# A two-layer Mamba-2 and attention trunk on eight cores: from 512-token blocks in a hand-written order to phases over the whole sequence in a list-scheduled order

## The chip, the cores and the metric

One Trainium2 chip, two dies of four cores. The program runs on all eight cores; each core computes one of the eight sequences of the batch (2048 tokens of 1024 features), and there is no traffic between cores. The metric is the device time of the slowest core, in microseconds (us). Engines: PE does matmuls (PEld its weight loads), DVE is the vector engine, ACT the scalar engine, POOL the GpSimd, SP issues transfers.

The program has a second, slower state: in some executions the cores of one die get a lower clock and take some per cent longer. Runs in that state are marked slow below, and only fast runs are compared.

## The reference, cut to what matters

The lines are shortened and put together by hand; the shapes are the reference's own.

```python
def reference(x, ...):                        # x: (8, 2048, 1024) float32
    # layer 1
    h = rms_norm(x, a_norm)
    x = x + mamba2_mixer(h, ...)              # in-projection 1024 -> 6176, out-projection 2048 -> 1024
    x = x + conv_ffn(x, f_norm[0], ...)
    # layer 2: keys and values shared, from the stream after layer 1
    k, v = split(rms_norm(x, kv_norm) @ w_kv + b_kv);  k = rotary(rms_norm(k, k_norm), positions)
    q = rotary(rms_norm(rms_norm(x, b_norm) @ w_q + b_q, q_norm), positions)
    x = x + sliding_window_sink_attention(q, k, v, sinks) @ w_o + b_o   # 16 query heads, 4 kv heads of 64, window 128
    x = x + conv_ffn(x, f_norm[1], ...)
    return x

def mamba2_mixer(h, ...):
    z, xBC, dt = split(h @ in_proj)                       # 2048, 2048 + 1024 + 1024, 32
    xs, B, C = split(silu(causal_dwconv(xBC, conv_w, conv_b)))   # 4 taps
    dt = softplus(dt + dt_bias);  A = -exp(A_log)
    # per chunk of L tokens, 32 heads of 64, 8 groups of B and C with state 128:
    #   y  = (C B^T * exp(a_cum[l] - a_cum[s]), causal) @ (dt x)  +  (C @ state) * exp(a_cum)
    #   state = state * exp(a_cum[last]) + B^T @ (exp(a_cum[last] - a_cum) dt x)
    y = ssd_chunked(xs, dt, A, B, C) + xs * D
    return group_rms_norm(y * silu(z), gnorm, 8) @ out_proj

def conv_ffn(x, g, w_in, conv_w, conv_b, w_down):          # 1024 -> 2 x 2816 -> 1024
    gate, val = split(rms_norm(x, g) @ w_in)
    return (silu(causal_dwconv(gate, conv_w, conv_b)) * val) @ w_down   # 3 taps
```

## The kernel before

It walks over four blocks of 512 tokens. Each block passes all stages: transposes of the input, norm, in-projection with convolution, SSD scan in chunks of 256 tokens, gated norm, out-projection, FFN, attention, FFN, output. The residual is feature-major (`xT`, features on partitions), so the sum of squares of a norm runs over partitions and takes a matmul with ones. All weights are loaded anew for every block. Engines work in the order in which the program is written; a helper records each operation and adds the semaphores.

```python
    for b in range(NBLK):                       # 4 blocks of 512 tokens
        ...
        rms_stats(lambda c: xT[:, c, :], 8, ones, 1.0 / D)
        ...
        for t in INP_ORDER:                     # in-projection, 512 columns at a time
            ...
        for ck in range(2):                     # two chunks of 256
            items = [(g, hh) for g in range(8) for hh in range(4)]   # one head at a time: s1, s2, s3 below

    def rms_stats(src_fn, nch, lhs, scale):
        bk = bank()
        for c in range(nch):
            ...                                 # squares, by ACT and DVE in turn
            K.mm(ps[:, bk, :], lhs, sqb[:, c % 2, :], start=(c == 0), stop=(c == nch - 1))
        K.act(lnb[:], ps[:, bk, :], AF.Ln, bias=epsb[:, 0:1], scale=scale)
        K.act(rstd[:], lnb[:], AF.Exp, scale=-0.5)

    def conv_taps(dst_acc, src_ps, raw, ntap, wname_fn, bname):
        K.act(dst_acc, src_ps, AF.Identity, bias=bname, scale=wname_fn(ntap - 1))
        for k in range(ntap - 2, -1, -1):       # raw: a copy of the bank in SBUF, with the last tokens of the block before
            K.stt(dst_acc, raw[:, k:k + TB], wname_fn(k), dst_acc, OP.mult, OP.add)

            def s2(i):                          # one head of the scan: three exponents, two products
                ...
                K.act(Erow[:, r, :]..., pa4[:, :, 0, :], AF.Exp)
                K.act(Eb[:, r, 0:256], ps[:, ba, 128:384], AF.Exp, bias=nacum[:, tl0, h:h + 1])
                K.act(Eb[:, r, 256:384], ps[:, ba, 384:512], AF.Exp, bias=nacum[:, tl1, h:h + 1])
                K.tt(Wt[:, r, :], CBb[:, g % 2, :], Eb[:, r, :], OP.mult)
                K.tt(Cs[:, r, :], CT[:, g, c0:c0 + 256], Erow[:, r, :], OP.mult)

                    # attention: one 128-query tile of one kv head
                    K.mm(ps[:, bs_, :]..., kT[P0:P0 + 64, pi, kt * 128:(kt + 1) * 128], qT_v[P0:P0 + 64, pi, :, qs], ...)
                    ...
                        K.mm(ps[P0:P0 + 64, bo_, :], vtok[:, kt, g * 64:(g + 1) * 64], pt, start=first, stop=last)
                        K.mm(ps[P0:P0 + 64, bd_, :], ones[:, 0:64], pt, start=first, stop=last)   # the denominator
                                    ...
                                    K.add("dve", (lambda e: e.reciprocal(dtot, dtot)), [dtot], [dtot])
```

The softmax here doesn't subtract the row's maximum and nothing guards it: scores larger than these inputs give would overflow.

## Time and profile before

| | before |
|---|---|
| runs (us) | 2699.05, 2696.23, 2768.55 |
| Mamba front, four blocks | 918 us |
| gated norm and out-projection | 182 us |
| FFNs, with output | 1050 us |
| attention | 554 us |
| moved by transfers | 248.37 MB |

Read the run's spread first: the third run is 2.6% longer than the other two, so it counts as slow. The stage sums are those of the prediction, cut from the trace where the PE work changes. Next, the head of the profile page: span, busy time of each engine (share of the span, number of instructions), and busy tenths in 40 slices of the span; PEclk is the granted clock of PE in tenths.

```profile
span 2704.2 us, 36898 instructions; the slowest of 8 cores (2688.7 to 2704.2 us)
...
PE 2282.5 (84%) x10240; PEld 980.2 (36%) x10240; DVE 1690.0 (62%) x3101; ACT 1271.6 (47%) x2806; POOL 457.2 (17%) x740
...
PE   5877997889786799878978679987897867998799
...
DVE  5887465653688655655368865565536896556553
...
PEclk8988997689898889668989888966898988896789
...
DMA packets 409782, 248.37 MB, mean 92 GB/s; under 512 B 85104, under 2 KB 404720, under 8 KB 409584
```

The four blocks can be seen as a pattern of ten slices that repeats: DVE high (8) in the front of each block, PE at 9 in the FFNs, and the clock down to 6 or 7 in each attention. Nearly all of the 409782 packets are under 2 KB.

### The profile page before, as it was taken

What the parts mean: (1) busy time and instruction counts of PE and PEld (TensorE: products, weight loads), DVE (VectorE), ACT (ScalarE), POOL (GpSimd) and SP (SyncE); (2) the same over time, 40 slices, a digit from 0 to 9 for tenths busy, and PEclk for the clock granted to TensorE, in tenths of its full rate; (3) what the DMA queues carried; (4) which work ended last, traced back from release to release, by engine and by line L of the source; (5) the groups of instructions that cost most, each with busy time, mean ns of one, the idle gap of its engine ahead of it and who ended that gap; (6) DMA issues with size and microseconds to landing.
All of it is one profiled execution on the core that took longest, in us unless ns stands there. A gap on an engine that the chain in (4) does not pass through costs nothing.

```text
span 2704.2 us, 36898 instructions; the slowest of 8 cores (2688.7 to 2704.2 us)
## 1 busy us (share of the span) xinstructions
PE 2282.5 (84%) x10240; PEld 980.2 (36%) x10240; DVE 1690.0 (62%) x3101; ACT 1271.6 (47%) x2806; POOL 457.2 (17%) x740
## 2 busy tenths in 40 slices
PE   5877997889786799878978679987897867998799
PEld 2443342234343334223434433422343433342234
DVE  5887465653688655655368865565536896556553
ACT  4667334342666542424266654242426665424342
POOL 1211222011120112101112011310111201131010
PEclk8988997689898889668989888966898988896789
DMA  8922999099780499709978049970997804997196
GB/s 141 125 33 51 117 133 109 8 116 120 135 122 3 84 122 122 83 9 119 119 133 123 2 84 123 123 80 12 114 123 137 122 2 50 122 121 82 24 117 109
DMA packets 409782, 248.37 MB, mean 92 GB/s; under 512 B 85104, under 2 KB 404720, under 8 KB 409584
## 3 DMA queue, kind: packets, MB, share of 16 engines
q0 software_dynamic: 403968, 227.31, 67.4%
q1 hardware_dynamic: 5616, 18.72, 2.0%
q8 instruction: 89, 1.46, 0.2%
q14 instruction: 109, 0.89, 0.1%
HBM read 464.88 MB, written 8.39 MB: 175 GB/s over the span
## 4 chain that ended last, share of the span: by engine, by line
PE 72%; DVE 13%; ACT 8%; issue 6%; DMA 0%; DVEq 0%; ACTq 0%; POOL 0%; SPq 0%; POOLq 0%
PE ps_ps L286 70%; DVE sb_accb L315 3%; DVE sb_Wt L305 2%; PE ps_ps L290 1%; ACT sb_sqb L302 1%; DVE sb_sqb L305 1%; ACT sb_accb L302 1%; ACT sb_lnb L302 1%; DVE sb_xdb L305 1%; ACT sb_Eb L302 1%; DVE sb_hT L1028 1%; ACT sb_Erow L302 1%; DVE sb_xcT L305 1%; ACT L302 1%; ACT sb_rstd L302 1%
## 5 line engine op out<-in xcount | busy, mean ns | idle before, releaser
L286 PE MATMUL ps_ps<-sb_hT,sb_wring 128*128 128x512 bf16 (+1 forms) x4384 | 1020.2, 394 | 64.1 <-DVE sb_hT L315 34.9
L315 DVE SCALAR_TENSOR_TENSOR sb_accb<-sb_rawb,sb_cst,sb_accb 128x512 f32<-128x512 f32 x736 | 543.5, 751 | 305.3 <-ACT sb_accb L302 241.7
L286 PEld LDWEIGHTS ps_ps<-sb_hT,sb_wring 128*128 128x128 bf16 (+1 forms) x4384 | 438.5, 100 | 643.8 <-issue 163.9
L302 ACT ACTIVATE sb_rawb<-ps_ps 128x512 f32<-128x512 f32 (+1 forms) x428 | 254.1, 594 | 494.6 <-PE ps_ps L286 494.0
L286 PE MATMUL ps_ps<-sb_zsT,sb_wring 128*128 128x512 bf16 x1856 | 443.1, 392 | 20.9 <-DVE sb_zsT L315 15.6
L324 POOL DMA_DIRECT2D sb_wring<-f_w_in x176 | 154.2, 878 | 1008.6 <-PE ps_ps L286 1008.6
L286 PEld LDWEIGHTS ps_ps<-sb_zsT,sb_wring 128*128 128x128 bf16 x1856 | 184.6, 100 | 260.2 <-issue 56.6
L302 ACT ACTIVATE sb_accb<-ps_ps,sb_cst 128x512 f32<-128x512 f32 x304 | 236.6, 778 | 20.0 <-DVE sb_accb L305 20.0
L305 DVE TENSOR_TENSOR sb_xT<-sb_xT,ps_ps 128x512 f32<-128x512 f32 x96 | 64.9, 686 | 268.7 <-PE ps_ps L286 267.5
L302 ACT ACTIVATE sb_Eb<-ps_ps,sb_nacum 128x256 bf16<-128x256 f32 (+1 forms) x512 | 197.8, 467 | 0.0
L286 PE MATMUL ps_ps<-sb_sqb,sb_cm 128*128 128x512 bf16 x220 | 96.5, 483 | 95.4 <-DVE sb_sqb L305 47.4
L302 ACT ACTIVATE sb_sqb<-sb_xT 128x512 bf16<-128x512 f32 x64 | 40.7, 636 | 285.6 <-PE ps_ps L286 235.5
L286 PE MATMUL ps_ps<-sb_xcT,sb_wring 128*128 128x512 bf16 x640 | 156.3, 391 | 13.2 <-DVE sb_xcT L305 9.5
L286 PE MATMUL ps_ps<-sb_Wt,sb_xdb 128*64 128x256 bf16 (+1 forms) x512 | 90.6, 260 | 72.6 <-DVE sb_Wt L305 72.5
L286 PE MATMUL ps_ps<-sb_cm 128*128 128x128 bf16 (+1 forms) x636 | 150.0, 304 | 0.0
L302 ACT ACTIVATE sb_zsT<-ps_ps 128x512 bf16<-128x512 f32 (+1 forms) x96 | 50.8, 602 | 187.0 <-PE ps_ps L290 146.4
L302 ACT ACTIVATE sb_Erow<-ps_ps 128x256 bf16<-128x256 f32 x256 | 108.2, 423 | 57.0 <-PE ps_ps L286 41.5
L286 PE MATMUL ps_ps<-sb_AH,sb_cm 128*128 128x512 bf16 x256 | 108.5, 424 | 18.8 <-DVE sb_xtk L318 18.5
L305 DVE TENSOR_TENSOR sb_Wt<-sb_CBb,sb_Eb 128x384 bf16<-128x384 bf16 x256 | 112.5, 440 | 14.7 <-ACT sb_Eb L302 14.5
L302 ACT ACTIVATE sb_xtk<-sb_accb 128x512 bf16<-128x512 f32 x176 | 112.1, 637 | 10.4 <-DVE sb_accb L315 10.3
L324 POOL DMA_DIRECT2D sb_wring<-f_w_down x64 | 54.1, 845 | 339.1 <-PE ps_ps L286 339.1
L310 DVE TENSOR_SCALAR sb_hT<-ps_ps,sb_esink 128x128 f32<-128x128 f32 x128 | 36.0, 344 | 114.2 <-PE ps_ps L286 114.2
(131 smaller groups left out, 2559.5 us busy)
## 6 DMA issues: line engine op xcount, KB each, us to landing
sb_wring<-f_w_in POOLq DMA_DIRECT2D x176, 512.0 KB, 9.2
sb_wring<-a_in_proj POOLq DMA_DIRECT2D x48, 1024.0 KB, 12.3
sb_wring<-f_w_down POOLq DMA_DIRECT2D x32, 768.0 KB, 9.0
sb_wring<-f_w_down POOLq DMA_DIRECT2D x32, 640.0 KB, 8.2
sb_wring<-a_out_proj POOLq DMA_DIRECT2D x16, 1024.0 KB, 9.3
sb_xdb<-x SPq DMA_DIRECT2D x16, 512.0 KB, 10.5
sb_wring<-w_q POOLq DMA_DIRECT2D x64, 128.0 KB, 13.8
sb_wring<-w_o POOLq DMA_DIRECT2D x32, 256.0 KB, 14.6
```

Of the source, the lines that this page charges most:

```text
L286: return self.add("pe", lambda e: e.matmul(out, lhsT, rhs, start=start, stop=stop), [lhsT, rhs] + ([] if start else [out]), [out])
L290: return self.add("pe", lambda e: e.transpose(out, in_, ident), [in_, ident], [out])
L302: return self.add("act", lambda e: e.activation(out, in_, func, **kw), rd, [out])
L305: return self.add(eng, lambda e: e.tensor_tensor(out, in0, in1, op), [in0, in1], [out])
L310: return self.add(eng, lambda e: e.tensor_scalar(out, in0, s1, None, op0), rd, [out])
L315: return self.add("dve", lambda e: e.scalar_tensor_tensor(out, in0, scalar, in1, op0, op1), rd, [out])
L324: return self.add(queue, lambda e: e.dma_start(out=out, in_=in_), [in_], [out], dma_sem=sem)
L1028: K.add("dve", (lambda e: e.reciprocal(dtot, dtot)), [dtot], [dtot])
```

## The change

The intent is one of structure: run each stage over the whole sequence before the next begins, so that it is filled and drained once and its weights are read less often; keep the residual token-major, so that a norm's sum comes out of the squaring activation; work on 1024 columns per instruction; put four heads into one exponent tile; and leave the order of instructions on each engine to a list scheduler that has a cost for each operation. PSUM has eight banks of 512 columns: in the front, banks 0 to 3 are two pairs for the projections, 4 to 7 serve the scan. To evacuate a bank is to copy its contents to SBUF, so that it can be written again.

The diff replaces nearly every line; its core, with cuts marked by dots:

```diff
-NBLK = T // TB
-    for b in range(NBLK):
+    units = [(g, h) for g in range(8) for h in range(2)]      # one B/C group, half of the sequence
+    for i, (g, h) in enumerate(units):
+        if i + 1 < len(units):
+            P_unit(*units[i + 1])                             # projections and convolution of the next unit
+        S_unit(g, h)                                          # scan of this one
+    def S_unit(g, h):
+        arload(g, h)
+        for q in range(2):                                    # 512 tokens: the "piece" of the text below
+            S_head(g, h, q)
+            while tails:
+                S_tail(*tails.pop(0))
+            S_core(g, h, q)
+            tails.append((g, h, q))
 ...
     P_unit:
-        K.act(rawb[:, r, 3:3 + TB], ps[:, bk, :], AF.Copy)
-        conv_taps(acc, ps[:, bk, :], rawb[:, r, :], 4, lambda k: C(f"cw{k}", j), C("cb", j))
+            K.act(acc, pp, AF.Identity, bias=C("cb", j), scale=C("cw3", j))     # pp: two banks, 1024 columns
+            for s in (1, 2, 3):
+                K.stt(acc[:, s:1024], pp[:, 0:1024 - s], C(f"cw{3 - s}", j), acc[:, s:1024], OP.mult, OP.add)
+            K.act(dst, acc, AF.Silu)
 ...
     S_head: transposes of x, of B, and the B-C products, all in bank 7, each evacuated before the next
     S_core:
-                K.act(Erow[:, r, :]..., AF.Exp)
-                K.act(Eb[:, r, 0:256], ..., AF.Exp, bias=nacum[:, tl0, h:h + 1])
-                K.act(Eb[:, r, 256:384], ..., AF.Exp, bias=nacum[:, tl1, h:h + 1])
+            K.mm(bank(4), LTb[...][:, q, c, :], RTb[r][:]..., start=True, stop=False)   # 4 heads of 128 columns
+            K.act(e_[:]..., bank(4), AF.Exp)
+            K.tt(W[c][:], e_[:], CBB[r][:, c, :].unsqueeze(1).to_broadcast([128, 4, 128]), OP.mult)
+                K.mm(ps[:, 7, k * 256:(k + 1) * 256], BtB[r][:, c, :], xddB[r][:, c, :], start=True, stop=True)   # states
+                K.copy(prevB[c][:], pF, eng="pool")
+                K.tt(st..., pF..., cdec[...], OP.mult, eng="pool")
+                K.tt(pF, st, ps[:, 7, k * 256:(k + 1) * 256], OP.add)
     S_tail:
+        pb = ps[:, 7, :].bitcast(BF16)...                     # transposes of the gated output, then into yT
 ...
     norm:
-            K.mm(ps[:, bk, :], lhs, sqb[:, c % 2, :], start=(c == 0), stop=(c == nch - 1))
+            K.act(junk[i % len(junk)], xv, AF.Square, scale=1.0 / 32.0, accum=ssq[:, r, i:i + 1])
 ...
     attention:
-                    K.mm(ps[:, bs_, :]..., kT[P0:P0 + 64, ...], qT_v[P0:P0 + 64, ...], start=True, stop=False)
+                        K.mm(s4, kz[:, g, kt * 128:(kt + 1) * 128], qv[:, pi, :, qs], start=True, stop=False)   # zero-padded keys
-                        K.mm(ps[P0:P0 + 64, bd_, :], ones[:, 0:64], pt, start=first, stop=last)
+                        K.mm(bank(pav), vA[:, kt, g, :], P, ...)      # values with a half of ones: pav = 6 + half
-                                    K.add("dve", (lambda e: e.reciprocal(dtot, dtot)), [dtot], [dtot])
+                K.act(dt_[:], dt_[:], AF.Ln)
+                K.act(dt_[:], dt_[:], AF.Exp, scale=-1.0)
 ...
     order of each engine:
-            for op in self.ops[eng]:                          # as written
+        self.schedule()                                       # ready list by priority, costs per operation
+            if is_w: deps.add(last writer of the bank); deps.update(readers of the bank)    # PSUM: by whole bank
```

The lines ahead of a colon and the last line are shortened by hand; all others are the kernels' own.

## The prediction

> **What bounds the kernel now.** I first read the spans and clocks of the cores (all eight 2689 to 2704 us, dies at 0.874 and 0.876: an undisturbed run), then the chain that ended last (it names PE for 72%, matmuls of one helper line), then busy time by stage. The stages are cut where the PE work changes; the second of the four 512-token blocks is: Mamba front (norm, in-projection, convolution, SSD scan), gated norm and out-projection, first FFN, attention, second FFN.
>
> ```profile
> PE 72%; DVE 13%; ACT 8%; issue 6%; DMA 0%; DVEq 0%; ACTq 0%; POOL 0%; SPq 0%; POOLq 0%
> ```
> ```profile
> core 0: us, PE busy (x) PEld busy (x) DVE busy (x) ACT busy (x) POOL busy (x), PEclk, DMA share, GB/s
> 679.00:904.20 225.20, 174.45 (x988) 88.22 (x987) 186.95 (x406) 148.91 (x349) 37.66 (x94) 0.89 0.49 76
> 904.20:949.30 45.10, 36.84 (x148) 14.56 (x147) 17.91 (x28) 17.64 (x31) 5.72 (x7) 0.81 0.82 134
> 949.30:1077.40 128.10, 121.68 (x538) 52.88 (x536) 72.03 (x110) 49.26 (x119) 33.03 (x38) 0.95 0.99 121
> 1077.40:1221.00 143.60, 114.57 (x334) 32.77 (x332) 81.99 (x140) 52.39 (x83) 12.83 (x17) 0.68 0.48 52
> 1221.00:1355.00 134.00, 125.86 (x575) 57.01 (x574) 62.28 (x90) 50.95 (x124) 25.08 (x29) 0.95 0.94 116
> ```
> ```profile
> 1258.00:1292.00 34.00, 34.00 (x159) 15.41 (x158) 20.48 (x30) 19.10 (x49) 6.95 (x8) 1.00 1.21 151
> 1122.00:1156.00 34.00, 31.70 (x69) 6.32 (x68) 17.67 (x34) 10.79 (x18) 0.00 (x0) 0.57 0.04 5
> ```
> Read matmul counts, not busy shares. In the FFN 159 matmuls of 512 columns take 34.00 us: 0.2138 us each at clock 1.00, as tight as it gets. In the attention PE is also "busy" for 31.7 of 34 us but does 69 matmuls, at clock 0.57. In the Mamba front DVE is busy for 187 of 225 us (83%), PE is not dense: DVE sets the pace. So three stages have three limits. Over the four blocks they sum to 918 us front, 182 gate and out-projection, 1050 FFN (with output), 554 attention: 2704.
>
> ```profile
> L315 DVE SCALAR_TENSOR_TENSOR sb_accb<-sb_rawb,sb_cst,sb_accb 128x512 f32<-128x512 f32 x736 | 543.5, 751 | 305.3 <-ACT sb_accb L302 241.7 <-ACT sb_rawb L302 18.2 <-DVE sb_accb L315 0.5
> L302 ACT ACTIVATE sb_accb<-ps_ps,sb_cst 128x512 f32<-128x512 f32 x304 | 236.6, 778 | 20.0 <-DVE sb_accb L305 20.0
> L305 DVE TENSOR_TENSOR sb_xT<-sb_xT,ps_ps 128x512 f32<-128x512 f32 x96 | 64.9, 686 | 268.7 <-PE ps_ps L286 267.5 <-PE ps_ps L290 1.2
> L1028 DVE RECIPROCAL sb_hT<-sb_hT 128x512 f32<-128x512 f32 x24 | 80.5, 3353 | 2.5
> L302 ACT ACT_TABLE_LOAD x24 | 30.8, 1283 | 23.2 <-PE ps_ps L286 12.5 <-DVE sb_accb L315 6.2 <-DMA sb_cst<-cst 4.4
> ```
> These groups give the prices. From pairs of sizes (472 ns at 256 and 751 at 512 for the three-operand op, 415 and 686 for the two-operand op) I extrapolate to 1024 columns: about 1.29 us and 1.22 us; an activation with two pointer operands 1.20 us, a plain one 1.02 us.
>
> **What the skill says.** "TensorE: Matmul & The Clock Gate", Part 1, has the clock at half or full by recent activity, and warns of 13/16 once three cores of a die are dense. The first agrees (69 against 159 matmuls in 34 us; clock 0.57 against 1.00); the second does not show here: eight cores run dense FFNs at 1.00. "ScalarE: Activation LUTs", What ACT_TABLE_LOAD costs, says about 1283 ns for each change of set; the row above reads 1283. "Advanced Engine Details and Errata", VectorE Performance Modes, says GPSIMD and two-port vector instructions block each other; here, beside a POOL multiply, one bf16 product takes twice its time:
> ```profile
> 211.46 0.66 POOL L305 TENSOR_TENSOR sb_stmp<-sb_prevF,sb_cdec 128x256 f32<-128x256 f32 x1 [20.17 <-DVE sb_prevF L305]
> 211.56 0.77 DVE L305 TENSOR_TENSOR sb_Wt<-sb_CBb,sb_Eb 128x384 bf16<-128x384 bf16 x1
> 212.46 0.35 DVE L305 TENSOR_TENSOR sb_Wt<-sb_CBb,sb_Eb 128x384 bf16<-128x384 bf16 x1
> ```
>
> **The change part by part.** *PE work hardly shrinks.* Before: 7904 streams of 512 columns, 832 of 256, 1216 of 128 and some 270 fp32 transposes; at 0.2138 us per 512, about 1900 us. After, counted from its instructions: 7076 of 512, 1408 of 256, and some 2,300 of 128 or fewer (transposes in bf16): about 1785. Gone are the 220 norm sums and half of the SSD's exponent streams; the projections (5760 of 512) stay. So of the 2704 us, 800 is PE idle or cold, and it is there that the change must earn.
>
> *FFN.* 4224 matmuls x 0.2138 = 903 us before and after. Before, eight FFNs each open with a norm (squares, ones-matmul, Ln, Exp, eight scalings) with PE waiting: 1050 - 903 = 147 us lost. After, there are four half-sequence passes; the second half's norm is issued within the first half's gate stage. I count 256 transposes (14 us) and four starts, four gate-to-down and two end bubbles at about 5 us: 903 + 14 + 45 = 962. DVE there needs 441 us, so it stays hidden.
>
> *Mamba front.* In-projection 332 us and SSD 170 us of PE, plus 15. DVE by its prices: 192 convolution steps x 1.29 = 247, their edges 24, 128 masked products of 512 53, state updates 54, output products 132, scaled inputs 39, norm scalings 29, 12 for the other tile, evacuations about 30, tables, norms and dt about 55: 683 us in all. The same sum for the old block is 206 us against a union of 187, as independent neighbours overlap by some 84 ns; with the same 0.91 that is 620. The old front had 753. So the front stays DVE-bound and shrinks by less than a fifth. New costs: POOL now has 256 small state operations (135 us by 0.67 and about 0.4) against 64, so collisions: about 25 us. Table changes on ACT: the fixed instruction order has about 107 in the front against 12; 107 x 1.283 = 137 us, ACT then about 535, still under DVE. In the dense part of the old front DVE was 87% occupied (148.8 of 170 us). (620 + 25) / 0.87 = 741, plus about 20 before the first tiles are in: 760, against 918.
>
> *Gate and out-projection.* The group norm moves into the scan (counted above); the 512 matmuls, 110 us, stay, some 30 us of them beside the last scan unit, and a bubble follows for the first FFN norm, whose scratch lies under the last gated tiles: 85, against 182.
>
> *Attention.* Heads of 64 become full 128-row and 128-column operands (zero-padded keys, values with a ones half), which drops the 124 separate denominator streams; the 3.35 us reciprocals become Ln and Exp. Per block PE has 61 us, ACT 57, DVE 58. The value banks are single, so each query tile passes add, Ln, Exp, multiply before the next values: about 4.5 to 5 us each, 8 per block, about 38. With norm 5, projections of k, v, q 20, a chain of 8, output 14, less 3 of overlap: 82 to 90 per block, 355 in all against 554.
>
> Sum: 760 + 85 + 962 + 355 = 2162. As the list scheduler may overlap more across stages than I allowed, I shade this to 2140.
>
> *Weights.* Read twice or three times rather than four times, in long rows: DMA share, about 1.0 in the old FFN, should halve. No old wait is for weights, so this earns nothing directly.
>
> **The rivals.** (a) Dense PE trips the power limit. If FFN ran at 13/16, 962 would become about 1170, the total 2350. Against it: 1.00 in every dense FFN window; the slow run of 2768.55 us shows the state exists. (b) The front stalls in one PSUM bank: transposes, B-C products, states and output tiles share bank 7, about 14 us for each 512 tokens without contention, 20 with DVE queues, so 40 us per unit against DVE's 42. If they add rather than overlap, the front takes 850 and the total 2240. (c) Table changes make ACT the bound if each drags a drain with it: front 820. (d) The scheduler does much better than a hand order: DVE 95% occupied, front 690; attention 300, limited by PE and ACT; total about 2020. (e) Attention stays cold as now: the 96 attention streams of a block at 0.5 us rather than 0.21 add about 15 us a block, total 2200.
>
> **Range and chances.** (b), (c) and (e) lean up, (d) down; 2010 to 2290 covers all but (a). To miss 2% faster (2645) all gains but one would have to fail. Faster 0.97, same 0.02, slower 0.01.
>
> **What would show it.** Right: FFN stretches at clock 1.00 with about 159 matmuls per 34 us for over 900 us; DVE at 85% or more through the first 750 us with ACT at about 70%; about 110 table loads; attention near 88 us per block at a clock above 0.8; DMA share about 0.5. Wrong: a front under 700 or over 830; attention over 105 a block; FFN clock of about 0.81; PE waiting on bank 7's evacuations.

## The result, and the profile after

Ratios are computed as the mean time of one kernel's fast runs over that of the other's fast runs of the same rounds, so they are not quite the ratio of the medians, which take in slow runs too.

| | before | after |
|---|---|---|
| runs (us) | 2699.05, 2696.23, 2768.55 (slow), 2729.83 (state not on record) | 2172.00, 2170.62, 2186.64, 2227.78 (slow) |
| median | 2714.44 | 2179.32 |

Ratio of the fast runs 0.805, 95% interval 0.7988 to 0.8112: faster. In the slow run of after, the cores of die 1 took 2191 to 2227 us at clocks of 0.935 to 0.94, those of die 0 2168 to 2171 at 0.97. The profiled run is a fast one (2172.00 us, cores 2167.0 to 2170.9).

The head of the page of after, the same lines as for before, and its chain:

```profile
span 2170.9 us, 31606 instructions; the slowest of 8 cores (2167.0 to 2170.9 us)
...
PE 1927.3 (89%) x10808; PEld 943.2 (43%) x10808; DVE 1315.6 (61%) x2112; ACT 1055.7 (49%) x1635; POOL 372.2 (17%) x609
...
PE   2878888888888899899999999788888899999999
...
DVE  4888788878887751665235532767667665225532
...
PEclk9898999999999999999999999999999999999999
...
DMA packets 47851, 148.63 MB, mean 68 GB/s; under 512 B 9808, under 2 KB 11088, under 8 KB 47696
...
PE 73%; DVE 12%; issue 7%; ACT 4%; DMA 1%; POOL 1%; SPq 0%; DVEq 0%; ACTq 0%; POOLq 0%
```

PE is busy 355 us less, and the clock is at 9 tenths or more in all but two slices. The chain looks as before (PE 73%), which shows how little a share over the whole span says; the stages say more. Busy time by stage (columns as in the prediction's table), cut on the slowest core where the PE work changes: start, front, last scan piece, out-projection, first FFN, attention, second FFN; then 34 us each from the middle of the front, of an FFN gate stage, and of the attention:

```profile
core 1: us, PE busy (x) PEld busy (x) DVE busy (x) ACT busy (x) POOL busy (x), PEclk, DMA share, GB/s
0.00:68.00 68.00, 21.47 (x132) 12.23 (x133) 31.96 (x79) 28.09 (x49) 14.57 (x29) 0.92 0.73 185
68.00:737.00 669.00, 559.21 (x4158) 325.63 (x4157) 561.99 (x1018) 503.22 (x815) 125.79 (x254) 0.95 0.13 26
737.00:794.30 57.30, 54.09 (x400) 27.56 (x398) 39.74 (x81) 29.79 (x76) 20.07 (x40) 1.00 0.73 171
794.30:871.70 77.40, 77.40 (x359) 34.66 (x356) 15.82 (x23) 1.47 (x3) 7.38 (x14) 1.00 0.70 126
871.70:1345.60 473.90, 466.52 (x2244) 214.96 (x2244) 220.34 (x279) 130.64 (x144) 49.94 (x81) 0.99 0.43 74
1345.60:1695.60 350.00, 282.28 (x1285) 113.28 (x1282) 231.05 (x363) 244.02 (x430) 111.22 (x117) 0.96 0.36 63
1695.60:2170.90 475.30, 466.30 (x2241) 214.88 (x2240) 214.70 (x270) 118.43 (x121) 43.20 (x75) 0.99 0.47 89
476.00:510.00 34.00, 29.22 (x206) 15.48 (x204) 26.69 (x49) 24.89 (x43) 8.28 (x17) 0.95 0.10 18
1156.00:1190.00 34.00, 34.00 (x160) 15.41 (x158) 20.10 (x25) 10.77 (x11) 2.64 (x5) 1.00 0.44 75
1462.00:1496.00 34.00, 27.32 (x114) 9.62 (x113) 24.12 (x37) 28.77 (x55) 8.87 (x9) 1.00 0.33 63
```

| stage, us | before | predicted | after |
|---|---|---|---|
| Mamba front | 918 | 760 | 794.3 |
| gated norm and out-projection | 182 | 85 | 77.4 |
| FFNs, with output | 1050 | 962 | 949.2 |
| attention | 554 | 355 | 350.0 |
| sum | 2704 | 2162, shaded to 2140 | 2170.9 |

So attention gave the most (204 us), then the front (124), the gate and out-projection (105) and the FFNs (101). In the FFN 160 matmuls in 34 us against 159: the dense part is what it was, and the gain is in the norms and bubbles around it. In the attention window the clock is 1.00 and there are 114 matmuls where before had 69. In the front three engines are busy most of the time at once: of 669 us, PE is busy 84%, DVE 84%, ACT 75%.

The groups with the new prices and the new table loads (the first column after the count is busy time, then the mean in ns, then the idle time before):

```profile
L254 ACT ACT_TABLE_LOAD x110 | 141.1, 1283 | 56.2 <-PE ps L229 39.1
...
L269 DVE SCALAR_TENSOR_TENSOR acc_121<-ps,cst,acc_121 128x1023 f32<-128x1023 f32 (+2 forms) x96 | 122.3, 1274 | 6.0 <-ACT acc_121 L254 5.7
...
L254 ACT ACTIVATE facc_188<-ps,cst 128x1024 f32<-128x1024 f32 x44 | 53.0, 1204 | 146.5 <-PE ps L229 146.5
...
L258 DVE TENSOR_TENSOR u<-sg_190,ps 128x1024 bf16<-128x1024 bf16 x44 | 53.8, 1222 | 61.3 <-PE ps L229 57.0
```

The prices taken from pairs of sizes hold: 1.27 to 1.28 us against 1.29, 1.20 against 1.20, 1.22 against 1.22. Of the 110 table loads, 107 are in the front, as counted.

### The profile page after: what moved, and what is told of

The parts are those of the page before. It is cut to its first block, busy times and chain, and to the rows that moved or that the text cites. A ratio compares the mean times of both kernels' runs of the same rounds, so it can differ in the third digit from the quotient of the medians.

```text
span 2170.9 us, 31606 instructions; the slowest of 8 cores (2167.0 to 2170.9 us)
## 1 busy us (share of the span) xinstructions
PE 1927.3 (89%) x10808; PEld 943.2 (43%) x10808; DVE 1315.6 (61%) x2112; ACT 1055.7 (49%) x1635; POOL 372.2 (17%) x609
## 4 chain that ended last, share of the span: by engine, by line
PE 73%; DVE 12%; issue 7%; ACT 4%; DMA 1%; POOL 1%; SPq 0%; DVEq 0%; ACTq 0%; POOLq 0%
PE ps L229 71%; DVE acc_121 L269 3%; PE ps L234 2%; DMA xin_90<-x 1%; DVE acc_122 L269 1%; DVE prevF_149 L258 0%; DVE att L258 0%; DVE prevF_150 L258 0%; ACT hq L295 0%; POOL prevB_156 L285 0%; SPq L308 0%; POOL rs L258 0%; DVE yn_163 L264 0%; DVE yg_160 L258 0%; ACT dtot_208 L254 0%
## 5 line engine op out<-in xcount | busy, mean ns | idle before, releaser
L254 ACT ACT_TABLE_LOAD x110 | 141.1, 1283 | 56.2 <-PE ps L229 39.1
L269 DVE SCALAR_TENSOR_TENSOR facc_188<-ps,cst,facc_188 128x1023 f32<-128x1023 f32 x88 | 112.8, 1282 | 70.4 <-ACT facc_188 L254 69.6
L269 DVE SCALAR_TENSOR_TENSOR facc_189<-ps,cst,facc_189 128x1023 f32<-128x1023 f32 x88 | 112.8, 1282 | 68.0 <-ACT facc_189 L254 67.2
L269 DVE SCALAR_TENSOR_TENSOR acc_121<-ps,cst,acc_121 128x1023 f32<-128x1023 f32 (+2 forms) x96 | 122.3, 1274 | 6.0 <-ACT acc_121 L254 5.7
L254 ACT ACTIVATE facc_188<-ps,cst 128x1024 f32<-128x1024 f32 x44 | 53.0, 1204 | 146.5 <-PE ps L229 146.5
L269 DVE SCALAR_TENSOR_TENSOR acc_122<-ps,cst,acc_122 128x1023 f32<-128x1023 f32 (+2 forms) x96 | 122.1, 1272 | 0.0
L254 ACT ACTIVATE sg_191<-facc_189 128x1024 bf16<-128x1024 f32 x44 | 46.5, 1056 | 126.5 <-DVE facc_189 L269 126.5
L254 ACT ACTIVATE sg_190<-facc_188 128x1024 bf16<-128x1024 f32 x44 | 46.5, 1057 | 123.7 <-DVE facc_188 L269 123.7
L229 PE MATMUL ps<-cm 128*128 128x512 bf16 x252 | 98.4, 390 | 0.0
L258 DVE TENSOR_TENSOR u<-sg_190,ps 128x1024 bf16<-128x1024 bf16 x44 | 53.8, 1222 | 61.3 <-PE ps L229 57.0
L258 DVE TENSOR_TENSOR x_73<-x_73,ps 128x512 f32<-128x512 f32 x8 | 5.5, 686 | 135.5 <-PE ps L229 135.5
L254 ACT ACTIVATE facc_189<-ps,cst 128x1024 f32<-128x1024 f32 x44 | 53.0, 1204 | 70.8 <-PE ps L229 70.8
L258 DVE TENSOR_TENSOR u<-sg_191,ps 128x1024 bf16<-128x1024 bf16 x44 | 53.7, 1221 | 53.4 <-PE ps L229 51.9
L258 DVE TENSOR_TENSOR x_65<-x_65,ps 128x512 f32<-128x512 f32 x8 | 5.5, 685 | 110.9 <-PE ps L229 110.9
L229 PE MATMUL ps<-hT,wr_61 128*128 128x512 bf16 x256 | 65.4, 389 | 5.0 <-DVE acc_122 L269 3.2
L229 PE MATMUL ps<-wr_64,u 128*128 128x512 bf16 x288 | 68.6, 379 | 0.8 <-DVE u L258 0.8
L229 PE MATMUL ps<-wr_63,u 128*128 128x512 bf16 x288 | 68.6, 379 | 0.2 <-DVE u L258 0.2
L229 PE MATMUL ps<-wr_60,u 128*128 128x512 bf16 x288 | 67.4, 379 | 0.2 <-DVE u L258 0.2
L229 PE MATMUL ps<-hF_182,wr_61 128*128 128x512 bf16 x288 | 64.6, 380 | 0.3 <-issue 0.2
L229 PE MATMUL ps<-hF_182,wr_63 128*128 128x512 bf16 x288 | 64.3, 380 | 0.2 <-issue 0.2
L229 PE MATMUL ps<-wr_62,u 128*128 128x512 bf16 x272 | 63.8, 379 | 0.4 <-DVE u L258 0.4
L229 PE MATMUL ps<-hF_182,wr_64 128*128 128x512 bf16 x288 | 63.6, 379 | 0.0
```

What stands on the lines that cost most here:

```text
L229: return self.add("pe", lambda e: e.matmul(out, lhsT, rhs, start=start, stop=stop, **kw), [lhsT, rhs] + ([] if start else [out]), [out], c)
L254: return self.add("act", lambda e: e.activation(out, in_, func, **kw), rd, wr, c, table=table)
L258: return self.add(eng, lambda e: e.tensor_tensor(out, in0, in1, op), [in0, in1], [out], c)
L269: return self.add("dve", lambda e: e.scalar_tensor_tensor(out, in0, scalar, in1, op0, op1), rd, [out], self._c_dve(out, [in0, in1], "stt"))
```

## The experiments

The predicted stage sums came out within 10% each, but two of them rest on reasons that a right sum doesn't prove: that DVE sets the pace of the front, and that a chain on the single value banks sets that of the attention. The experiments go there first. My theory for the front was DVE; the rivals were the table loads on ACT and the shared PSUM bank 7. All kernels are the changed kernel with one edit, two of them with a second one on top. An edit changes the scheduler's list, so a stage can move by some us for that alone; how much is seen below. Stage times of core 1, cut as above, except that the last column ends with the last matmul; the time is that of the profiled run:

| kernel | time, us | front | out-proj. | FFN 1 | attention | FFN 2 |
|---|---|---|---|---|---|---|
| after | 2172.00 | 794.3 | 77.4 | 473.9 | 350.0 | 471.2 |
| no SiLU tables in the front | 2196.13 | 788.7 | 77.6 | 473.9 | 350.6 | 472.0 |
| one tap fewer | 2163.30 | 777.4 | 78.9 | 474.1 | 351.4 | 471.7 |
| tail in bank 6 | 2145.86 | 752.6 | 89.3 | 474.1 | 350.8 | 472.2 |
| x tiles staged | 2194.79 | 809.1 | 77.4 | 473.9 | 349.5 | 471.0 |
| tail after the core | 2176.00 | 786.6 | 81.9 | 473.9 | 351.3 | 472.0 |
| four value banks | 2203.09 | 789.3 | 77.4 | 473.9 | 381.9 | 469.6 |
| 64-row operands | 2192.09 | 788.3 | 77.4 | 473.9 | 369.5 | 471.3 |
| short weight rows | 2171.95 | 791.2 | 77.4 | 473.9 | 349.2 | 471.9 |
| bank 6 and early head | 2140.09 | 753.0 | 88.0 | 474.0 | 348.0 | 471.7 |
| program order | 3359.69 | 1465.5 | 120.9 | 511.5 | 723.6 | 516.9 |
| bank 6 and one tap fewer | 2108.33 | 716.9 | 86.9 | 473.9 | 347.8 | 471.6 |

Stages that an edit doesn't touch agree with after within 2.2 us, program order left out, apart from the front of kernels whose edit is elsewhere (788.3 to 791.2 against 794.3) and the out-projection, part of which runs beside the last scan piece: what the front gains, the out-projection can lose. So for edits of the front look at the sum of both columns too: 871.7 in after, 856.3 with one tap fewer, 841.9 with the tail in bank 6, 868.5 with the tail after the core, 886.5 with x staged, 803.8 with bank 6 and one tap fewer. The kernel before, run beside them, took 2700.43, 2703.91 and 2693.93 us.

The length of the front also mixes its start with its repeated part. A second measure leaves the start out. The scan has 32 pieces, with four masked products (tile `W`) each on DVE; the time on core 1 from the first masked product of piece 5 to that of piece 29 is that of 24 pieces:

| kernel | 24 pieces, us | piece 5 starts at, us |
|---|---|---|
| after | 513.5 | 214.3 |
| edits outside the front (three kernels) | 507.8 to 511.1 | 213.6 to 215.0 |
| no SiLU tables | 521.0 | 202.9 |
| one tap fewer | 511.5 | 200.8 |
| x tiles staged | 508.6 | 234.4 |
| tail after the core | 521.4 | 207.5 |
| tail in bank 6, and its repeat | 482.2, 482.3 | 214.6, 217.0 |
| bank 6 and early head | 494.6 | 205.6 |
| bank 6 and one tap fewer | 460.4 | 199.3 |

Only the kernels with the tail in bank 6 stand apart.

### No SiLU tables in the front

SiLU becomes a plain copy, so that ACT needs one table only. Its output is wrong, which doesn't matter for the time.

```diff
-            K.act(dst, acc, AF.Silu)
+            K.act(dst, acc, AF.Copy)
-            K.act(zB[u][:, t4 * 4:(t4 + 1) * 4, :].rearrange("p a n -> p (a n)"), pair(tl), AF.Silu)
+            K.act(zB[u][:, t4 * 4:(t4 + 1) * 4, :].rearrange("p a n -> p (a n)"), pair(tl), AF.Copy)
```

> The changed kernel with the SiLU of the Mamba front (convolution tiles and gate) replaced by a plain copy on the same engine, so that the front needs one activation set only; wrong result on purpose. Removes about 104 of the 110 table loads (133 us of ACT) and the idle around them. Theory DVE-bound (DVE busy 84% of the steady part, 42.7 us per unit of the 16): front 794 -> 775 to 794 us, DVE occupancy unchanged. Rival ACT/table loads: front -> 700 to 740 us, DVE occupancy over 90%. I lean to something between, about 760.

Measured: 5 table loads instead of 107 in the front; between 68 and 737 us ACT was busy 391 us rather than 503. The front took 788.7 us, 5.6 less. (The time of the whole run is longer because two cores, 2 and 3, ran at a mean clock of 0.954, with 0.93 and some 500 us in the second FFN; the others took 2164 to 2167.) A fifth of ACT's work removed brings less than 1%, and the 24 pieces take 521.0 us, no less than in after: table changes don't set the pace, rival (c) falls. The 760 us to which the expectation leaned did not come.

### One tap fewer

One of the three DVE convolution steps is dropped: 64 steps at 1.27 us are 81 us, with their edges some 87 us of DVE. Its output is wrong, which doesn't matter for the time.

```diff
-            for s in (1, 2, 3):
+            for s in (1, 2):
```

> The changed kernel with one of the three convolution taps of the Mamba front left out; wrong result on purpose. Takes 64 vector operations of 1.27 us and 32 small ones (0.2 us) from DVE, 87 us, and nothing from PE or POOL. Theory DVE-bound: front 794 -> 700 to 715 us. Rival chain through PSUM bank 7 or ACT: front falls by under 25 us. In between means that no single engine sets the pace.

Measured: the front took 777.4 us, 17 less. Were DVE the limit, most of the 87 us would have come back. By the second measure most of even these 17 belong to the start: piece 5 began 13.5 us earlier, and the 24 pieces after it, which hold some 65 of the 87 us, took 511.5 us against 513.5. So "the front stays DVE-bound" is wrong as a statement of cause. Where the time went is seen in the waits of DVE between 100 and 680 us (line waited at, who released it: us in total, times, longest). After:

```profile
DVE prevF_149 L258 <- PE ps L229: 17.1, 7, 3.6
...
DVE prevF_150 L258 <- PE ps L229: 13.3, 7, 3.6
...
DVE yT L296 <- PE ps L229: 8.2, 2, 6.2
```

One tap fewer:

```profile
DVE yT L296 <- PE ps L234: 45.8, 6, 8.4
DVE yT L296 <- PE ps L229: 39.0, 7, 7.1
```

`yT` is the evacuation of the tail, `prevF` the state update; both read what PE wrote in bank 7. With less to do, DVE stands for 85 us, 13 times, at the tail's evacuation: the time saved turned into a wait there. PE, too, waits longer for readers of bank 7: in the same stretch 28.9 us for ACT's evacuation of B, where after has 5.4. That points to bank 7. It does not prove it, as the tail also waits for the gated norm of its piece.

### The tail in bank 6

```diff
     def S_tail(g, h, q):
-        pb = ps[:, 7, :].bitcast(BF16).rearrange("p (ch c n) -> p ch c n", ch=2, c=4)
+        pb = ps[:, 6, :].bitcast(BF16).rearrange("p (ch c n) -> p ch c n", ch=2, c=4)
```

> The changed kernel with the transposes of the output tiles moved from PSUM bank 7 (shared with the head transposes, B-C products and states) to bank 6; the result must stay right. Rival bank-7 chain: that bank is relieved of about 2 of 14 us per 512 tokens, front -30 to -60 us. Theory DVE-bound: within 10 us of 794.

Measured: results correct, 2145.86 us (fast; its other run 2407.65, slow, with die 0 at a clock of 0.82 to 0.83). The front took 752.6 us, 41.7 less; the out-projection, part of which now lies after the front, 11.9 more. Together the two stages are 29.8 us shorter, and the 24 pieces took 482.2 us rather than 513.5. This is the largest gain that a single edit brought to the front, from one digit. It was repeated, with three rounds beside before:

> The one-line move of the tail's transposes from bank 7 to bank 6, timed in three rounds against the kernel before. If the first look was no accident (2145.86 us in a fast run, front 752.6 us): fast runs of 2140 to 2150 us, ratio to the kernel before 0.79 to 0.80, some 1.2 per cent under the changed kernel's 2170.6 to 2186.6 us. The rival, that re-listing alone moved the front by luck, makes no other forecast for the same instruction list; what it would need is a fast run at 2165 or more, which would say the first look was a lucky chip. Slow runs, if any, at 2380 to 2420 us on one die at a clock of about 0.82.

Measured: 2150.31, 2146.33, 2147.49 and 2147.89 us, all fast; before 2701.44, 2697.55 and 2696.12 (fast) and four slow runs of 2846.82 to 2910.84. Ratio of the fast runs 0.7962, 95% interval 0.7939 to 0.7985. By medians (2147.69 against the 2172.00 of after's three fast runs) the version is 1.1% faster than the changed kernel; these two were not timed in the same rounds. The repeat has the same instruction list, so it can't tell what the bank does from what the new list does. What speaks for the bank is that no new list without the move brought the 24 pieces below 507.8 us. The waits of DVE in the same stretch of this run:

```profile
DVE t L258 <- PE ps L229: 12.1, 14, 1.5
...
DVE yT L296 <- PE ps L229: 8.6, 3, 5.5
...
DVE prevF L258 <- PE ps L229: 2.6, 7, 0.7
```

The 30.4 us for which the state updates waited for PE are 2.6 now. On the slowest core DVE is busy 90% of the time between 68 and 690 us, where it was 84% between 68 and 737 in after (columns as in the stage table):

```profile
68.00:690.00 622.00, 517.18 (x3978) 309.61 (x4039) 556.88 (x994) 474.55 (x784) 132.24 (x253) 0.97 0.14 26
```

The Trainium skill, "PSUM — Partial Sum Buffer", section "PSUM bank collisions raise a hardware error", says that the hardware doesn't arbitrate when two engines use one bank on the same partitions, and that semaphores must guard by bank and group of partitions, or more simply by bank. This kernel does so: its dependencies go by whole bank. Thus the tail's transposes, the head's, the B-C products and the states, which share no data, form one line at bank 7. No run here shows a collision. The waits fit a price of that guard, but the wait of the state updates alone doesn't measure it: with the early head below it is back at 19.3 us, and with the tail after the core it is 0.6 us without a gain.

### The tail after the core

Is it only the place of the tail in that line? Here the tail keeps bank 7 but is emitted after the scan core, not before it.

```diff
             S_head(g, h, q)
+            S_core(g, h, q)
             while tails:
                 S_tail(*tails.pop(0))
-            S_core(g, h, q)
             tails.append((g, h, q))
```

> The changed kernel with the output-tile transposes of one 512-token piece issued after the next piece's core instead of before it, still in PSUM bank 7; the result must stay right. Theory bank-order: in bank 7 the next piece's states wait for these transposes, which wait for the whole gated-norm chain of the piece before, so that pieces follow one another at 21.3 us each; freed of that, front 794 -> 740 to 755 us (at least the 42 us that moving them to bank 6 gave) with DVE at 88% or more. Rival (bank 7 is simply occupied too long, whatever the order): within 10 us of 794. Rival (in-order engines, not banks): within 10 us.

Measured: correct, 2176.0 us fast (2253.3 slow); front 786.6 us, 7.7 less. The 24 pieces took 521.4 us, and at piece 29 this kernel was 1.2 us behind after: the 7.7 us come from the last four pieces, not from the pace. In the waits of DVE between 100 and 680 us the state updates hardly wait for PE any more (0.6 us), but the evacuation of the B-C products, which also lie in bank 7, waits 9.8 us and the masked product 15.5. PE, in turn, waits for the readers of bank 7, between 100 and 670 us (`xk` is the first evacuation of the head, `CB` that of the B-C products):

```profile
PE ps L234 <- DVE xk L293: 20.8, 11, 2.5
PE ps L229 <- DVE prevF L258: 15.5, 12, 1.8
PE ps L229 <- DVE CB L293: 11.5, 12, 1.1
```

In after the largest such entry for that stretch is 5.6 us, again for `xk`. So the place of the tail in the line isn't it: the waits move to other users of the bank. Of the two edits only the one that takes work out of the bank helped.

### Bank 6 and an early head

If bank 7 still limits, starting the next piece's head before the present core should gain again.

```diff
-    def S_unit(g, h):
-        arload(g, h)
+    def S_unit(g, h, nxt, first):
+        if first:
+            arload(g, h)
+            S_head(g, h, 0)
         for q in range(2):
-            S_head(g, h, q)
+            if q == 0:
+                S_head(g, h, 1)
+            elif nxt is not None:
+                arload(*nxt)
+                S_head(*nxt, 0)
 (and the tail in bank 6)
```

> As f_bank6 (output-tile transposes in bank 6), and the head of the next 512-token piece (its transposes and B-C products, all in bank 7) is issued before the core of the present one instead of after it; the result must stay right. Theory bank 7 as a serial chain: its uses for the next piece no longer stand behind the states of this one; front 753 -> 715 to 735 us, DVE over 90% in the steady part. Rival (bank 7 is no longer the limit once the tails are out): 745 to 760. Note that moving things by itself shifts the scheduler's list: f_xstage and f_late show 8 to 15 us from that, so under 15 us says nothing.

Measured: correct, 2140.09 us fast (2402.46 slow, die 0 at 0.82 to 0.83); front 753.0, the same as with bank 6 alone. By the second measure piece 5 began 9 us earlier and the 24 pieces took 12 us more (494.6), so the early head gained nothing for the pace. That fits bank 7 no longer holding the front, but this new order also brought waits of its own (19.3 us of the state updates for PE).

### Bank 6 and one tap fewer

Is it DVE then, at 90%? Both edits. Its output is wrong, which doesn't matter for the time.

> As f_bank6 with one convolution tap left out as in f_tap3 (87 us of DVE work; wrong result on purpose). With the tails in bank 7 that tap gave 17 us of 87. Theory (the bank hid the DVE bound): now 50 to 75 us, front 753 -> 680 to 705. Rival (the front is a loop of dependent steps on in-order engines, in which DVE load still counts for little): 15 to 30 us, front 725 to 740.

Measured: front 716.9 us, 35.7 less than with bank 6 alone, from the same 87 us of DVE work. Without the move it was 17. In the 24 pieces the tap now gives 21.8 us of some 65, where it gave 2. So with the bank relieved, DVE counts for more, but still for less than half of what is taken from it. Between 68 and 690 us PE is now the fullest, 88% on the slowest core, with DVE at 83%:

```profile
68.00:690.00 622.00, 547.59 (x4245) 328.91 (x4311) 516.07 (x974) 451.04 (x793) 145.23 (x273) 0.98 0.17 35
```

There is no single engine: three of them at 73 to 88%, each working in a fixed order, wait for one another in turn. Which loop of waits sets the pace of a piece (21 us per 512 tokens of a group) I have not found.

### The x tiles staged

The first in-projection matmul starts at 45.7 us, where I had estimated 20. The chain of after in its first 46 us has the cause in one line (start, duration, what), the eighth tile of x:

```profile
9.68 29.51 DMA xin_90<-x
```

All 16 tiles of x are requested without waiting for any; before asked for four, and they were there after 12.60 us. The edit holds each of the second eight back until one of the first has landed, by a one-column copy into it.

```diff
     for i in range(16):
+        if i >= 8:
+            K.copy(x0[i][:, 0:1], x0[i - 8][:, 0:1], eng="pool")
         K.dma("sp", x0[i][:], x_d[i * 128:(i + 1) * 128, :], f"x{i}")
```

> The changed kernel with each of the second eight tiles of x loaded only after one of the first eight has landed (one POOL copy of a column sets the order); the result must stay right. In the changed kernel all sixteen tiles share the DMA engines and the first in-projection matmul starts at 45.7 us. Theory: the late start is part of the front's miss of 34 us; the first in-projection matmul moves to about 30 us and the whole falls by 10 to 16 us. Rival: the start is not on the path, because DVE work only moves: no change (under 4 us).

Measured: correct, 2194.79 us. It failed to do what it was for: as one tile lands the next is requested, and SP sent its sixteen requests between 2.9 and 39.1 us, where in after it had sent them between 2.9 and 35.2 anyway; the eighth tile landed at 38.2 us and the first matmul came at 44.3. The front took 809.1 us, 14.8 more, though only its start was touched. The trace shows where: in the new list SP requests the decay rows of the scan (tile `LT`) from 99.1 us on, in after from 71.1; DVE stands for them once for 12.1 us at 103.9, and the first masked product comes at 145.9 us, not at 127.1. The 24 pieces are not slower (508.6 us). With the 3 to 6 us that the front moved under edits of other stages, it says that a new list alone can move the front by 3 to 15 us, so that smaller effects (the SiLU tables, the tail's order) can't be told from none, and that the 17 us of the missing tap is barely more. The 42 and 36 us (30 and 38 with the out-projection) stand clear of it.

### Four value banks

For the attention I had a chain on the single value banks: 4.5 to 5 us for each query tile, 8 per block. Here the value tiles alternate between two pairs of banks, at the cost of one bank for projections and one for scores.

```diff
-        b = rb[0] % 3
+        b = rb[0] % 2
-                    pav = 6 + half
+                    pav = 4 + 2 * (nl % 2) + half
-                        sb_ = 3 + ac_[0] % 3
+                        sb_ = 2 + ac_[0] % 2
 (and the two readers of the value bank alike)
```

> The changed kernel with four PSUM banks for the attention values (alternating by query tile) instead of two, two for scores instead of three and two for projections instead of three; the result must stay right. Theory of the prediction (each query tile passes add, Ln, Exp, multiply before the next values): attention 350 -> 305 to 325 us. Rival (PE, ACT and DVE are each near 70% and the rest is mixing): 340 to 355, or longer because the projections now have fewer banks.

Measured: correct, 2203.09 us, attention 381.9, which is 31.9 more. The theory would have it shorter. The edit also takes a bank each from the projections and the scores (before the value products PE now waits mostly for the exponentials of the scores, 13.9 us in 35 waits), so it doesn't measure the chain alone; but in after itself, PE waits for the last step of the chain, the product that frees a value bank, only this long in the whole attention:

```profile
PE ps L229 <- DVE att L258: 7.5, 11, 1.5
```

7.5 us in 11 waits, two of which (1.9 us) are waits of the output projection, and not 38 us per block. The sum was right; for the reason the runs show no support, though an edit that gives the values more banks and takes none away wasn't run.

### 64-row operands

Before's attention ran at a clock of 0.68 over the stage in its second block (0.57 in the 34 us shown in the prediction), after's at 0.96. Is it that before used half of the array (64 rows of keys, 64 columns of values)? Here the scores use 64 rows, and the value product is split into two of 64 columns.

```diff
-                        K.mm(s4, kz[:, g, kt * 128:(kt + 1) * 128], qv[:, pi, :, qs], start=True, stop=False)
+                        K.mm(s4, kz[64 * half:64 * half + 64, g, ...], qv[64 * half:64 * half + 64, pi, :, qs], start=True, stop=False)
-                        K.mm(bank(pav), vA[:, kt, g, :], P, start=(ti == 0), stop=(ti == len(tiles) - 1))
+                        for r0 in (0, 64):
+                            K.mm(ps[r0:r0 + 64, pav, :], vA[:, kt, g, r0:r0 + 64], P, start=(ti == 0), stop=(ti == len(tiles) - 1))
```

> The changed kernel with the attention operands of the kernel before: scores from 64 rows, values and denominators as two products of 64 columns; 124 streams of 512 more; the result must stay right. Theory clock-by-active-array: granted clock in the attention falls from 0.96 to under 0.8 and the attention grows from 350 to 410 us or more. Rival (the clock follows time with matmuls, whatever their size): clock stays over 0.9 and the attention grows by the added streams at most, 0 to 27 us.

Measured: correct, 2192.09 us, attention 369.5 (19.5 more) at a clock of 0.94. The 124 added streams of 512 columns alone are 124 x 0.2138 = 26.5 us, so the added work covers it, and the clock hardly falls. Half-array operands did not make PE cold here. Why before's attention was cold stays open. In the 34 us of the prediction its 69 matmuls start 0.49 us apart on average, where dense ones take 0.2138 us; whether so thin a stream keeps the clock low no run shows.

### Short weight rows

The prediction said that long weight rows earn nothing directly. Here the FFN-in weights come in rows of 1 KB, as before.

```diff
-            [_kview(np.concatenate([wf[:, j * 128:(j + 1) * 128], wf[:, FFN + j * 128:FFN + (j + 1) * 128]], axis=1))
+            [np.concatenate([wf[:, j * 128:(j + 1) * 128], wf[:, FFN + j * 128:FFN + (j + 1) * 128]], axis=1)
 (and the load of a tile with 8 rows per partition instead of one)
```

> The changed kernel with the FFN input weights left in rows of 1 KB in HBM, as in the kernel before, instead of rows of 8 KB per partition; the result must stay right. Theory of the prediction (packing earns nothing, no wait is for weights): within 6 us of 2171, DMA share of the FFN gate stages up from about 0.43 to over 0.6. Rival: the loads come late and each FFN gate stage (152 us) grows by 5 us or more.

Measured: correct, 2171.95 us, first FFN 473.9 us as in after; from 1150 to 1190 us the DMA share is 0.62 rather than 0.45. More transfer work, no time: the step was right.

### Program order

All parts of the change, but every engine works in the order in which the program is written, as before did; only which of ACT and DVE takes an evacuation is still the scheduler's choice. One execution.

```diff
+        order = {e: sorted(order[e], key=lambda o: o.idx) for e in self.ENGS}
+        for op in ops:
+            op.start = float(op.idx)
         self.ops = order
```

> The changed kernel with every engine taking its instructions in the order in which the program writes them, and not in the list scheduler's; the result must stay right. Theory (the overlap of projection and scan in the front is the scheduler's work): each of the 16 units takes a projection of 22 to 26 us and then two scan pieces of 15 to 20 us one after another, front 900 to 1050 us; attention 370 to 420; FFN within 20 us of 474 each; in all 2330 to 2500 us, so a good half of the change's gain. Rival (the buffers and the phases give the gain, the order little): under 2230 us.

Measured: correct, 3359.69 us, 25% slower than the 2693.93 of before on the same chip; every stage is longer, the front 1.8 times and the attention 2.1 times. Both dies are alike (3339.1 and 3346.5 us), and where PE is dense the clock is 1.00. In the middle of the front, and in a gate stage:

```profile
680.00:714.00 34.00, 16.62 (x112) 10.54 (x112) 12.84 (x29) 11.90 (x23) 3.88 (x8) 0.67 0.00 1
1900.00:1934.00 34.00, 34.00 (x159) 15.43 (x158) 20.08 (x25) 10.78 (x11) 2.64 (x5) 1.00 0.43 75
```

112 matmuls in 34 us of the front where after has 206, all engines below half, at a clock of 0.67: units follow one another instead of overlapping. I had not thought that the order alone outweighs the whole gain (1188 us against some 530). Before had its overlap written in by hand, item by item; this program leaves it to the scheduler, so the two can't be judged apart.

## Why the prediction was right or wrong, point by point

- **Time and range.** 2140 predicted, 2170.62 to 2186.64 in fast runs, inside the range and faster by far more than 2%. The unshaded sum, 2162, was closer. (The DVE list of the front adds to 675 us, not 683; with that the front would have been about 754 and the sum about 2156.) The shade for a scheduler that "may overlap more across stages than I allowed" had no row behind it, and there was no such gain.
- **FFN: right, with its reason.** 949.2 us against 962. 160 matmuls in 34 us at clock 1.00; the 4224 matmuls at 0.2138 us take 903, so 46 us were left for transposes and bubbles where I had 59.
- **Gated norm and out-projection: right.** 77.4 us against 85.
- **Attention: sum right, reason not.** 350.0 us against 355, at the clock I had hoped for (0.96). But nothing shows that the step "each query tile passes add, Ln, Exp, multiply before the next values" fills it: PE waits 7.5 us for the end of that chain in all. The same sum is made of many small waits and of ACT, PE and DVE at 70, 81 and 66% busy. Rival (e), cold PE, did not occur. (Its 96 streams at 0.5 rather than 0.21 us are 28 us a block, not 15, unless half of it is hidden.)
- **Front: near, for the wrong reason.** 794.3 us against 760. The start is 26 us of the 34: first matmul at 45.7 us, not 20. The rest of the front took 748.6 us, against my 741. The DVE sum was good too (634 us busy against 645). What failed is the step "so the front stays DVE-bound": 87 us less DVE work gave 17, and next to nothing in the 24 repeated pieces, while one user less in bank 7 gave 31 us there. The near hit of the sum was thus in part luck: pieces that wait on each other through a bank took about as long as DVE's work divided by 0.87. PE was also fuller than said: 517 us by columns, 635 by the trace (21.47 + 559.21 + 54.09). Of these some 33 us are 155 matmuls of the out-projection, and part is a clock of 0.95; but in the 669 us PE was as full as DVE, which the prediction did not see.
- **Rivals.** (b), the shared bank 7, was the nearest: moving one of its users gave 42 us, more than any other single edit of the front, though it did not make the front as long as I had said for it (850). Its sign did show, if weakly: between 100 and 680 us of after PE waited some 22 us for evacuations and state updates that read bank 7. (c), table changes: 107 of them, as counted, and their removal gave 6 us, no more than edits elsewhere. (a), a lower clock when PE is dense, did not occur in the FFNs of after (0.99 to 1.00 on all cores of the profiled run). That the slow run of 2768.55 us was this state, as the prediction has it, isn't shown: that run has no clocks on record. (d) fell with the measured 794.
- **Weights: right.** The DMA share of the gate stage fell from 1.21 to 0.44, and giving part of it back cost nothing.
- **Order.** The prediction gave the scheduler 22 us. Taking it away costs 1188 (one execution). The prediction did not ask what the new program would be without it.

## What to carry to other kernels

A stage sum that comes out right doesn't prove the limit it was computed from: take work away from the engine you name, and see whether the stage follows. Where three engines are at 75 to 90%, look for what makes unrelated work queue, such as a PSUM bank with four users; the wait shows up at an innocent instruction, and moving one user may cost one digit. And where a scheduler lists anew after every edit, a stage can move by 3 to 15 us in 790 without the cause that was meant, so don't read smaller effects; time the repeated part apart from the start, which here told a gain in pace (31 us) from a gain in the start (13 of 17 us).

## What the Trainium skill lacked or had wrong

- "TensorE: Matmul & The Clock Gate", Part 1, advises to budget 13/16 of the clock for dense work on all cores of a die. Here all eight cores run FFNs of some 470 us at 0.99 to 1.00 in the profiled run of after, and in the profiled runs of the edits too, but for two: cores 2 and 3 of the kernel without SiLU tables had 0.93 in the second FFN, and with program order, where the FFNs take 511 to 518 us, it was 0.95 to 0.97. In slow runs one die does fall near that figure (0.82 to 0.83 over the whole run with the tail in bank 6, 2407.65 us against 2145.86, 12% longer; the other die at 0.98), and before falls from 0.87 to 0.77 to 0.81 (2846.82 to 2910.84 us against 2697). The page doesn't say that the same program has both states.
- "ScalarE: Activation LUTs", What it computes, mentions the accumulator output without a cost. In after it comes with a separate instruction (ACTIVATION_READ_ACCUMULATOR) of 187 ns for each such activation (`gjunk` alone has 128 of them, 24 us in the front); the prediction doesn't name them.
- No page has the time of a power on POOL: in after it takes 759 ns for 2 columns, where a product of 256 columns takes 612 to 631.
